# The last quarter of k for four row tiles: 32x32 blocks on VectorE in place of transposes on TensorE

## Chip, cores and metric

One Trainium2 chip, one core. The metric is device microseconds of one execution, lower is better. A core has TensorE (PE; its weight loads are listed as PEld), VectorE (DVE), ScalarE (ACT), GpSimd (POOL) and SyncE (SP), which here only issues transfers. Each engine works through its own list of instructions in order. SP's and GpSimd's transfers go to DMA queues.

## What is computed

```python
def reference(a, b, gamma, beta, eps):        # a, b: 2048 x 2048, float32
    x = np.matmul(a, b)
    mean = np.mean(x, axis=-1, keepdims=True)
    var = np.var(x, axis=-1, keepdims=True)
    normalized = (x - mean) / np.sqrt(var + eps)
    return (gamma * normalized + beta).astype(np.float32)
```

A product of two 2048×2048 matrices, then a layer norm over each row of the result.

## The kernel before

**Tiling.** A is cut into 16 row tiles i (or g) of 128 rows, k into 16 steps t of 128, B's columns into four quarters q of 512. One product `mm(i, q, t)` (line 139) multiplies A's transposed block (128×128, fp16) with a block of B (128×512, fp16) into one of the eight PSUM banks. TensorE needs A with k on the partitions, so every block of A has to be transposed. k is dealt to the steps so that four steps share a quarter c of k (512 values): value p·4 + t of quarter c lies on partition p of step 4c + t. B is loaded and kept in that order (`b_rows`, line 68), as is A's transposed tile `at[i]`, 128 × 16 steps × 128 (line 128).

**Loads of B.** `load_b(t, h)` (line 74) fetches half h of B's row tile t: 128 partitions × 1024 float32, 512 KB, into one of eight buffers. `cast_left` and `cast_right` (lines 79 and 84) turn a tile into fp16, one half of the columns on VectorE, the other on ScalarE. It is complete in SBUF as fp16 and is read by all row tiles.

**Two ways to transpose A.** Row tiles 0 to 3 go by pieces: 16 pieces n, piece n being row tile n mod 4 and quarter n // 4 of k (`pieces`, line 89). `load_first(n)` (line 91) fetches one with the rows on the partitions (128 × 512 float32, one transfer of 256 KB, 2 KB a row); `cast_first` (line 100) makes it fp16 on VectorE and reorders it; `turn_first` (line 105) transposes it on TensorE, four times 128×128, into a PSUM bank; `keep_first` (line 110) copies that to `at[g]` on VectorE. Row tiles 4 to 15 go by quadrants: `load_tile` (line 114) makes eight transfers of 64 KB, each filling 32 partitions with 32 rows r of each of the four blocks of 32 rows, and 128 values of k (512 bytes a run); `cast_tile` (line 122) makes fp16 on ScalarE, and `transpose_part` (line 130) turns 32×32 blocks on VectorE for one quarter of k, writing straight to `at[i]`.

**Order of the start.** The order of all engines is written out by hand (line 297). SP loads (lines 312 to 335): pieces 0 to 3 with B's left tiles 0 to 3, each piece of A one ahead of B's; the right tiles 0 to 3 with pieces 4 to 7; then B's left tiles 4 to 15, each of tiles 4 to 11 followed by one of the pieces 8 to 15; then B's right tiles 4 to 15, with row tile 4 in quadrants among the last of them.

TensorE computes row tiles 0 to 3 in four stages. The first quarter of k (t = 0 to 3, `K1 = 4`) is done for B's left half, then for the right half; the partial sums are put by in SBUF (`put_by`, line 150). Then the rest of k (t = 4 to 15) is done for the left half and the right half, and the partial sums are added (`add_up`, line 157). A half of four row tiles fills all eight banks, `left` or `right`; a transposed piece needs a bank too, so the eighth (`late`) joins the others once its bank is free of transposes. In the third stage (lines 428 to 445) step t keeps the piece before, casts the next, casts B's tile t + 1, and makes five products, four transposes and two products; when t = 12 is done, the late bank catches up on t = 4 to 12, and a closing loop (lines 446 to 451) takes t = 13, 14, 15 bank by bank and adds up. Then come row tiles 4 to 14 one by one (line 483) and the last one in narrower spans. The products of `warm_up` (line 303) only keep TensorE at work; nobody reads them.

Of the kernel before, what the change touches and what calls it, by code (L numbers as in the profile page):

```python
# [9 lines left out]
FP32 = mybir.dt.float32  # L10
FP16 = mybir.dt.float16
# [4 lines left out]
def kernel(  # L16
# [18 lines left out]
    nc = tc.nc  # L35
    P = 128
# [3 lines left out]
    n_kt = K // P  # L40
# [3 lines left out]
    G = 4  # L44
# [4 lines left out]
    firstp = ctx.enter_context(tc.tile_pool(name="firstp", bufs=4))  # L49
    first16 = ctx.enter_context(tc.tile_pool(name="first16", bufs=2))  # L50
    a16p = ctx.enter_context(tc.tile_pool(name="a16p", bufs=6))
# [17 lines left out]
    a_pieces = a.rearrange("(s r) (c q k) -> q c r s k", r=32, c=4, q=4)  # L69

    bnst, x_of, mv_of, rs_of, at = {}, {}, {}, {}, {}
    a_in, b_in, t_of, tile_in, part = {}, {}, {}, {}, {}

    def load_b(kt, h, queue=None):
        w = bigp.tile([P, NH], FP32, tag="big", name=f"w{kt}_{h}")
        (queue or nc.sync).dma_start(w, b_rows[kt // 4, kt % 4][:, ds(h * NH, NH)])
        b_in[kt, h] = w

    def cast_left(kt):
        w = b_in.pop((kt, 0))  # L80
        nc.vector.tensor_copy(b16[:, kt, 0:NB], w[:, 0:NB])
        nc.scalar.copy(b16[:, kt, NB:NH], w[:, NB:NH])

    def cast_right(kt):
        w = b_in.pop((kt, 1))
        nc.vector.tensor_copy(b16[:, kt, NH:NH + NB], w[:, 0:NB])
        nc.scalar.copy(b16[:, kt, NH + NB:N], w[:, NB:NH])
# [3 lines left out]
    def load_first(n):  # L91
        g, c = pieces[n]
        if n % 2 == 0:
            a_in[n + 1] = firstp.tile([P, 2, 4 * P], FP32, tag="first", name=f"f{g}_{c}")
            a_in[n] = a_in[n + 1][:, 0]
        else:
            a_in[n] = a_in[n][:, 1]
        nc.sync.dma_start(a_in[n], a[ts(g, P), ts(c, 4 * P)])

    def cast_first(n):  # L100
        h = first16.tile([P, P, 4], FP16, tag="h", name=f"h{n}")
        nc.vector.tensor_copy(h.rearrange("m p t -> m (p t)"), a_in[n])
        a_in[n] = h

    def turn_first(n):
        t_of[n] = psum.tile([P, 4, P], FP16, tag="c_ps", bufs=8, name=f"t_ps{n}")
        for t in range(4):
            nc.tensor.transpose(t_of[n][:, t, :], a_in[n][:, :, t], ident)

    def keep_first(n):  # L110
        g, c = pieces[n]
        nc.vector.tensor_copy(at[g][:, ds(4 * c, 4), :], t_of[n])  # L112

    def load_tile(i, h, queue):
        f = firstp.tile([P, 2, 4, P], FP32, tag="first", name=f"p{i}_{h}")
        for c in (0, 1):
            for q in range(4):
                queue.dma_start(  # L118
                    f[ds(32 * q, 32), c], a_pieces[q, 2 * h + c][:, ds(4 * i, 4)])
        tile_in[i, h] = f  # L120

    def cast_tile(i, h):
        a16 = a16p.tile([P, 2, 4, P], FP16, tag="a16", name=f"a{i}_{h}")
        nc.scalar.copy(a16, tile_in.pop((i, h)))  # L124
        tile_in[i, h] = a16
# [10 lines left out]
    def bank(i, q):  # L136
        x_of[i, q] = psum.tile([P, NB], FP32, tag="c_ps", bufs=8, name=f"ps_{i}_{q}")

    def mm(i, q, kt, lo=0, hi=n_kt):
        nc.tensor.matmul(  # L140
            x_of[i, q], at[i][:, kt, :], b16[:, kt, ds(q * NB, NB)],
            start=(kt == lo), stop=(kt == hi - 1),
        )
# [6 lines left out]
    def put_by(i, q):  # L150
        part[i, q] = xpool.tile([P, NB], FP32, tag="x_sb", name=f"x_{i}_{q}")
        if q % 2:
            nc.vector.tensor_copy(part[i, q], x_of[i, q])
        else:
            nc.scalar.copy(part[i, q], x_of[i, q])
# [141 lines left out]
    with tc.manual_schedule(engines=order):  # L297
# [5 lines left out]
        def warm_up(n):  # L303
            for _ in range(n):
                nc.tensor.matmul(w_ps, warm[:, 0:P], warm, start=True, stop=True)  # L305
# [3 lines left out]
            base=0, pattern=[[-1, P]], channel_multiplier=1,  # L309
        )  # L310
        K1 = 4
        load_first(0)
        for t in range(K1):
            if t + 1 < K1:
                load_first(t + 1)
            load_b(t, 0)
        for t in range(K1):
            load_b(t, 1)
# [2 lines left out]
        load_first(2 * K1 - 1)  # L321
        for t in range(K1, n_kt):
            load_b(t, 0)
            if K1 + t < n_kt:
                load_first(K1 + t)
        for t in range(K1, n_kt - 2):
            load_b(t, 1)
        load_tile(4, 0, nc.sync)
        for t in range(n_kt - 2, n_kt):
            load_b(t, 1)  # L330
        load_tile(4, 1, nc.sync)
        for h in (0, 1):
            load_tile(5, h, nc.sync)
# [6 lines left out]
        left = [(g, q) for g in range(G) for q in (0, 1)]  # L340
        right = [(g, q) for g in range(G) for q in (2, 3)]
        early, late = left[:-1], left[-1]
# [1 line left out]
            new_at(g)  # L344


        def step(t, gs):
            for g in gs:
                for q in (0, 1):
                    mm(g, q, t, 0, K1)  # L350

        warm_up(10)
        cast_first(0)
        turn_first(0)
        cast_first(1)
        warm_up(1)
        keep_first(0)
        turn_first(1)
        warm_up(2)
        keep_first(1)  # L360
        cast_left(0)
        for x in early[:4]:
            bank(*x)
        step(0, (0, 1))
        cast_first(2)
        turn_first(2)
        warm_up(2)
        keep_first(2)
        cast_left(1)
        for x in early[4:]:  # L370
            bank(*x)
        step(0, (2,))
        step(1, (0, 1))
        cast_first(3)
        turn_first(3)
        step(1, (2,))
        keep_first(3)
        bank(*late)
        step(0, (3,))
        step(1, (3,))  # L380
        cast_left(2)
        step(2, range(G))
        cast_left(3)
        for j, (g, q) in enumerate(left):
            mm(g, q, K1 - 1, 0, K1)
            put_by(g, q)
            if j == 3:
                cast_right(0)
        cast_right(1)


        early, late = right[:-1], right[-1]
# [13 lines left out]
        waits = list(range(K1))  # L406
        for j, (g, q) in enumerate(early):
            mm(g, q, K1 - 1, 0, K1)
            put_by(g, q)
            if j in (4, 6):  # L410
                n = K1 + j // 2
                turn_first(n)
                keep_first(n)
            if j in (1, 3, 5):
                mm(*late, waits.pop(0), 0, K1)
            if j == 2:
                cast_left(K1)
            if j == 5:
                cast_first(2 * K1)
        for t in waits:  # L420
            mm(*late, t, 0, K1)
        put_by(*late)
# [2 lines left out]
        early, late = left[:-1], left[-1]  # L425
        for g, q in early:
            bank(g, q)
        for t in range(K1, n_kt - 3):
            n = K1 + t
            if t > K1:  # L430
                keep_first(n - 1)
            if K1 < t and n < n_kt:
                cast_first(n)
            cast_left(t + 1)
            for g, q in early[:5]:
                mm(g, q, t, K1)
            if n < n_kt:
                turn_first(n)
            for g, q in early[5:]:
                mm(g, q, t, K1)  # L440
        bank(*late)
        for t in range(n_kt - 2, n_kt):
            cast_left(t)
        for t in range(K1, n_kt - 3):
            mm(*late, t, K1)
        for j, (g, q) in enumerate(left):
            for t in range(n_kt - 3, n_kt):
                mm(g, q, t, K1)
# [96 lines left out]
```

## Time and profile before

| | |
|---|---|
| median of 3 runs | 244.94 us (244.73 to 245.02) |
| the profiled execution, its own time | 244.94 us |
| its span in the profile | 243.2 us, mean granted TensorE clock 0.991 |
| DMA traffic | 52.66 MB, mean 217 GB/s |

The page's second part shows the span in 40 slices of 6.08 us. Digits are busy tenths; PEclk is the granted TensorE clock, DMA the mean busy share of 16 DMA engines:

```profile
PE   8899999999999999999999999999999999999960
PEld 3434554444444444444444444444444444446440
DVE  1657864894499999998999899998999895966962
ACT  2364434543325230461908255370917391020020
POOL 0000000000786599788866807693760000000011
PEclk9999999999999999999999999999999999999996
DMA  5999999995999768585675626473674222030405
GB/s 154 412 402 401 400 402 409 406 343 165 245 222 315 198 181 277 183 270 136 243 208 204 228 97 241 158 281 89 216 213 170 98 86 89 31 142 0 175 0 173
```

A column is one moment. The first nine columns, some 55 us, are the loading of B and of the first row tiles; the four stages of row tiles 0 to 3 end at 68.8 us.

### The profile page before, as it was taken

What the parts mean: (1) busy time and instruction counts of PE and PEld (TensorE: products, weight loads), DVE (VectorE), ACT (ScalarE), POOL (GpSimd) and SP (SyncE); (2) the same over time, 40 slices, a digit from 0 to 9 for tenths busy, and PEclk for the clock granted to TensorE, in tenths of its full rate; (3) what the DMA queues carried; (4) which work ended last, traced back from release to release, by engine and by line L of the source; (5) the groups of instructions that cost most, each with busy time, mean ns of one, the idle gap of its engine ahead of it and who ended that gap; (6) DMA issues with size and microseconds to landing.
All of it is one profiled execution on the core that took longest, in us unless ns stands there. A gap on an engine that the chain in (4) does not pass through costs nothing.

```text
span 243.2 us, 3383 instructions
## 1 busy us (share of the span) xinstructions
PE 232.3 (96%) x1135; PEld 108.3 (45%) x1135; DVE 198.3 (82%) x373; ACT 92.7 (38%) x165; POOL 89.4 (37%) x168
## 2 busy tenths in 40 slices
PE   8899999999999999999999999999999999999960
PEld 3434554444444444444444444444444444446440
DVE  1657864894499999998999899998999895966962
ACT  2364434543325230461908255370917391020020
POOL 0000000000786599788866807693760000000011
PEclk9999999999999999999999999999999999999996
DMA  5999999995999768585675626473674222030405
GB/s 154 412 402 401 400 402 409 406 343 165 245 222 315 198 181 277 183 270 136 243 208 204 228 97 241 158 281 89 216 213 170 98 86 89 31 142 0 175 0 173
DMA packets 22129, 52.66 MB, mean 217 GB/s; under 512 B 4448, under 2 KB 9056, under 8 KB 21856
## 3 DMA queue, kind: packets, MB, share of 16 engines
q1 hardware_dynamic: 16704, 41.74, 47.6%
q0 software_dynamic: 5120, 10.50, 16.6%
q10 hardware_dynamic: 288, 0.21, 0.3%
q8 instruction: 9, 0.15, 0.2%
q14 instruction: 8, 0.07, 0.1%
HBM read 35.65 MB, written 16.78 MB: 216 GB/s over the span
## 4 chain that ended last, share of the span: by engine, by line
PE 91%; DVE 3%; DMA 2%; SPq 0%; issue 0%; DVEq 0%
DMA w_0_109<-in_b_dram 2%; PE ps_0_2051 L140 1%; PE ps_1_1374 L140 1%; PE ps_0_998 L140 1%; PE ps_last_2337 L229 1%; PE ps_last_2318 L229 1%; PE ps_3_2233 L140 1%; PE ps_2_2215 L140 1%; PE ps_0_2178 L140 1%; PE ps_1_1966 L140 1%; PE ps_0_1943 L140 1%; PE ps_2_1870 L140 1%; PE ps_3_1770 L140 1%; PE ps_1_1728 L140 1%; PE ps_0_1705 L140 1%; PE ps_0_1589 L140 1%
## 5 line engine op out<-in xcount | busy, mean ns | idle before, releaser
L214 ACT ACTIVATE junk<-b_93 128x1024 f16<-128x1024 f16 x32 | 33.7, 1054 | 0.5
L118 POOL DMA_DIRECT2D p_0_232<-in_a_dram x8 | 4.9, 622 | 59.0 <-DMA w_1_199<-in_b_dram 59.0
L268 POOL TENSOR_TENSOR u_last_n<-u_last_n,gamma_b 128x128 f32<-128x128 f32 x1 | 0.5, 453 | 54.1 <-ACT u_last_n L267 54.1
L229 PEld LDWEIGHTS <-at_2050 128*128 128x128 f16 x96 | 8.8, 98 | 5.4
L140 PEld LDWEIGHTS <-at_412 128*128 128x128 f16 x64 | 6.1, 98 | 9.0 <-issue 2.1
L140 PEld LDWEIGHTS <-at_997 128*128 128x128 f16 x64 | 6.3, 98 | 7.5
L140 PEld LDWEIGHTS <-at_1350 128*128 128x128 f16 x64 | 6.3, 98 | 7.5
L140 PEld LDWEIGHTS <-at_1826 128*128 128x128 f16 x64 | 6.3, 98 | 7.5
L140 PEld LDWEIGHTS <-at_1942 128*128 128x128 f16 x64 | 6.3, 98 | 7.5
L140 PEld LDWEIGHTS <-at_988 128*128 128x128 f16 x64 | 6.3, 98 | 7.5
L140 PEld LDWEIGHTS <-at_1115 128*128 128x128 f16 x64 | 6.3, 98 | 7.5
L140 PEld LDWEIGHTS <-at_1466 128*128 128x128 f16 x64 | 6.3, 98 | 7.5
L140 PEld LDWEIGHTS <-at_1588 128*128 128x128 f16 x64 | 6.3, 98 | 7.6
L140 PEld LDWEIGHTS <-at_1704 128*128 128x128 f16 x64 | 6.2, 97 | 7.6
L140 PEld LDWEIGHTS <-at_837 128*128 128x128 f16 x64 | 6.2, 97 | 7.6
L140 PEld LDWEIGHTS <-at_1228 128*128 128x128 f16 x64 | 6.2, 97 | 7.6
L140 PEld LDWEIGHTS <-at_413 128*128 128x128 f16 x64 | 6.2, 98 | 7.6
L140 PEld LDWEIGHTS <-at_415 128*128 128x128 f16 x64 | 6.2, 98 | 6.7 <-DVE at_415 L112 0.6
L140 PEld LDWEIGHTS <-at_414 128*128 128x128 f16 x64 | 6.1, 98 | 6.6 <-DVE at_414 L112 0.6
L305 PE MATMUL w_ps<-warm 128*128 128x512 f16 x15 | 6.3, 565 | 1.2 <-DVE warm L298 1.2
L118 POOL DMA_DIRECT2D p_0_358<-in_a_dram x8 | 4.3, 550 | 8.0 <-ACT a_0_1608 L124 5.5
L118 POOL DMA_DIRECT2D p_0_394<-in_a_dram x8 | 4.3, 548 | 5.5 <-ACT a_0_1846 L124 5.5
(575 smaller groups left out, 644.0 us busy)
## 6 DMA issues: line engine op xcount, KB each, us to landing
gamma_b<-in_gamma_dram SPq DMA_DIRECT2D x1, 1024.0 KB, 7.1
beta_b<-in_beta_dram SPq DMA_DIRECT2D x1, 1024.0 KB, 11.3
f_0_106<-in_a_dram SPq DMA_DIRECT2D x2, 256.0 KB, 4.1
w_0_109<-in_b_dram SPq DMA_DIRECT2D x1, 512.0 KB, 5.7
f_0_111<-in_a_dram SPq DMA_DIRECT2D x2, 256.0 KB, 6.4
w_0_113<-in_b_dram SPq DMA_DIRECT2D x1, 512.0 KB, 6.7
w_0_116<-in_b_dram SPq DMA_DIRECT2D x1, 512.0 KB, 7.7
w_0_118<-in_b_dram SPq DMA_DIRECT2D x1, 512.0 KB, 8.2
```

The costliest lines, as they stand in the source:

```text
L118: queue.dma_start(f[ds(32 * q, 32), c], a_pieces[q, 2 * h + c][:, ds(4 * i, 4)])
L140: nc.tensor.matmul(x_of[i, q], at[i][:, kt, :], b16[:, kt, ds(q * NB, NB)], start=(kt == lo), stop=(kt == hi - 1),)
L214: nc.scalar.activation(junk, b16[:, kt, ds(h * NH, NH)], ActFn.Copy, accum_out=b_sum[:, h, kt:kt + 1])
L229: nc.tensor.matmul(x[:, 0:w], at[last][:, t, :], b16[:, t, ds(lo, w)], start=(t == 0), stop=(t == n_kt - 1))
L268: nc.gpsimd.tensor_tensor(y, y, gamma_b[:, ds(lo, w)], AluOp.mult)
L305: nc.tensor.matmul(w_ps, warm[:, 0:P], warm, start=True, stop=True)
```

## The change

Row tiles 0 to 3 get their last quarter of k (pieces 12 to 15) in the second way: four transfers of 64 KB into quadrants (`load_fourth`), a cast on ScalarE and a transpose by 32×32 blocks on VectorE (`turn_fourth`). Their loads stand where the pieces stood, behind B's left tiles 8 to 11. In the third stage the transposes on TensorE end with step 7; the late bank catches up after step 8, and steps 9 to 12 run over all eight banks, each turning one row tile's last quarter.

The first stage is written anew: B's left tile t now follows A's piece t instead of piece t + 1, and the order of casts, transposes, products and warm-ups is another (19 warm-up products for 15). The cast of piece 8 moves from the second stage into the third's first step.

```diff
+    def load_fourth(g):
+        if g % 2 == 0:
+            tile_in[g, 3] = firstp.tile([P, 2, 4, P], FP32, tag="first", name=f"p{g}_3")
+            tile_in[g + 1, 3] = tile_in[g, 3]
+        for q in range(4):
+            nc.sync.dma_start(
+                tile_in[g, 3][ds(32 * q, 32), g % 2], a_pieces[q, 3][:, ds(4 * g, 4)])
+
+    def turn_fourth(g):
+        a16 = a16p.tile([P, 4, P], FP16, tag="a16", name=f"a{g}_3")
+        nc.scalar.copy(a16, tile_in[g, 3][:, g % 2])
+        nc.vector.transpose(
+            at[g][:, ds(12, 4), :].rearrange("p t (j r) -> p j t r", r=32),
+            a16.rearrange("p j (k t) -> p j t k", t=4),
+        )
...
         K1 = 4
-        load_first(0)
         for t in range(K1):
-            if t + 1 < K1:
-                load_first(t + 1)
+            load_first(t)
             load_b(t, 0)
...
         for t in range(K1, n_kt):
             load_b(t, 0)
-            if K1 + t < n_kt:
+            if t < 2 * K1:
                 load_first(K1 + t)
+            elif t < 3 * K1:
+                load_fourth(t - 2 * K1)
...
-        cast_first(1)
-        warm_up(1)
-        keep_first(0)
-        turn_first(1)
-        warm_up(2)
-        keep_first(1)
-        cast_left(0)
...
+        warm_up(3)
+        for n in range(K1):
+            keep_first(n)
+            cast_left(n)
+            if n < K1 - 1:
+                cast_first(n + 1)
+            for x in early:
+                if x[0] == n:
+                    bank(*x)
+            todo = [
+                (g, q, t) for t in range(n + 1) for g, q in early
+                if g <= n and (g == n or t == n)
+            ]
+            if n == K1 - 1:
+                break
+            ahead = (2, 4, 6)[n]
+            for x in todo[:ahead]:
+                mm(*x, 0, K1)
+            if n == 0:
+                warm_up(2)
+            turn_first(n + 1)
+            for x in todo[ahead:]:
+                mm(*x, 0, K1)
+            if n < 2:
+                warm_up(2)
         bank(*late)
+        for g, q, t in todo[:K1 - 1]:
+            mm(g, q, t, 0, K1)
+        waits = list(range(K1))
+        for j, (g, q) in enumerate(early):
             mm(g, q, K1 - 1, 0, K1)
             put_by(g, q)
+            if j in (1, 3, 5):
+                mm(*late, waits.pop(0), 0, K1)
             if j == 3:
                 cast_right(0)
+        for t in waits:
+            mm(*late, t, 0, K1)
+        put_by(*late)
         cast_right(1)
...
-        for t in range(K1, n_kt - 3):
+        for t in range(K1, 2 * K1):
             n = K1 + t
             if t > K1:
                 keep_first(n - 1)
-            if K1 < t and n < n_kt:
-                cast_first(n)
+            cast_first(n)
             cast_left(t + 1)
             for g, q in early[:5]:
                 mm(g, q, t, K1)
-            if n < n_kt:
-                turn_first(n)
+            turn_first(n)
             for g, q in early[5:]:
                 mm(g, q, t, K1)
+        keep_first(3 * K1 - 1)
+        cast_left(2 * K1 + 1)
+        for g, q in early:
+            mm(g, q, 2 * K1, K1)
         bank(*late)
+        for t in range(K1, 2 * K1 + 1):
+            mm(*late, t, K1)
+        for t in range(2 * K1 + 1, n_kt - 3):
+            cast_left(t + 1)
+            turn_fourth(t - 2 * K1 - 1)
+            for g, q in left:
+                mm(g, q, t, K1)
         for t in range(n_kt - 2, n_kt):
             cast_left(t)
-        for t in range(K1, n_kt - 3):
-            mm(*late, t, K1)
```

More of the change, by code (lines that the diff above doesn't have):

```diff
@@ L344 @@
             new_at(g)
[L347 to L350, printed above, removed]
         warm_up(10)
@@ L354 @@
         turn_first(0)
-        cast_first(1)
-        warm_up(1)
-        keep_first(0)
-        turn_first(1)
-        warm_up(2)
-        keep_first(1)
-        cast_left(0)
[L362 to L377, printed above, removed]
-        bank(*late)
[L379 to L384, printed above, removed]
+        warm_up(3)
[23 more added lines that the diff above has]
+                warm_up(2)
+        bank(*late)
+        for g, q, t in todo[:K1 - 1]:
+            mm(g, q, t, 0, K1)
+        waits = list(range(K1))
+        for j, (g, q) in enumerate(early):
             mm(g, q, K1 - 1, 0, K1)
             put_by(g, q)
+            if j in (1, 3, 5):
+                mm(*late, waits.pop(0), 0, K1)
             if j == 3:
                 cast_right(0)
+        for t in waits:
+            mm(*late, t, 0, K1)
+        put_by(*late)
         cast_right(1)
@@ L417 @@
                 cast_left(K1)
-            if j == 5:
-                cast_first(2 * K1)
         for t in waits:
```

## The prediction

> **What bounds the kernel now.** I read the busy shares first, then busy time by stage, then the timeline of the stage that the change touches, then the transfers.
>
> ```profile
> span 243.2 us, 3383 instructions
> PE 232.3 (96%) x1135; PEld 108.3 (45%) x1135; DVE 198.3 (82%) x373; ACT 92.7 (38%) x165; POOL 89.4 (37%) x168
> ```
>
> TensorE is busy nearly throughout, so anything taken off it looks like a gain. By stage (length, then busy time of PE, PEld, DVE, ACT, POOL, granted clock, DMA share, GB/s):
>
> ```profile
> 24.96:42.78 17.82, 17.81 (x105) 8.91 (x104) 11.21 (x30) 6.52 (x12) 0.00 (x0) 1.00 1.03 404
> 42.78:47.96 5.18, 5.18 (x25) 2.35 (x24) 4.60 (x9) 2.55 (x5) 0.00 (x0) 1.00 1.03 410
> 47.96:68.84 20.88, 20.88 (x97) 9.39 (x96) 13.79 (x28) 7.49 (x11) 6.27 (x11) 1.00 0.95 252
> ```
>
> 24.96 to 42.78 us is the left half of B, steps t = 4 to 12, where the removed transposes sit. TensorE has no gap there, but neither have the transfers: share 1.03 at 404 GB/s. Two limits lie side by side. Which ends last is read where the stage ends:
>
> ```profile
> 31.07 0.43 DVE L81 CAST b_93<-w_0_148 128x512 f16<-128x512 f32 x1
> 33.01 0.43 DVE L81 CAST b_93<-w_0_152 128x512 f16<-128x512 f32 x1 [0.32 <-DMA w_0_152<-in_b_dram]
> ...
> 40.13 0.43 DVE L81 CAST b_93<-w_0_164 128x512 f16<-128x512 f32 x1 [0.52 <-DMA w_0_164<-in_b_dram]
> ...
> 41.41 0.43 DVE L81 CAST b_93<-w_0_166 128x512 f16<-128x512 f32 x1 [0.85 <-DMA w_0_166<-in_b_dram]
> 42.69 0.43 DVE L81 CAST b_93<-w_0_168 128x512 f16<-128x512 f32 x1 [0.85 <-DMA w_0_168<-in_b_dram]
> 42.78 0.81 PE L140 MATMUL ps_0_627<-b_93,at_412 128*128 128x512 f16 x3
> ```
>
> These casts start when their piece of B lands (VectorE sat idle for it). A 512 KB row tile of B alone takes 1.28 us (40.13 to 41.41 to 42.69); with a 256 KB piece of A between, 1.94 (31.07 to 33.01; 1.96 in the three steps after it), so such a piece of A costs 0.67. w_0_168 is the last left tile, t = 15. It is cast by 42.69 + 0.43 = 43.12. The closing loop takes t = 13, 14, 15 bank by bank: its first three products start at 42.78, and with 0.216 us between starts the third, the first to read t = 15, starts at 43.21. The margin is **0.09 us**. Everything behind it (5.18 of 5.18 us busy, then 20.88 of 20.88) is dense on TensorE, so a tile 15 that lands D later ends the kernel D − 0.09 later, however early TensorE is ready.
>
> **The change part by part.**
>
> Transposes on TensorE: 16 go. A step with them takes 1.73 us (timeline: t = 7 starts at 30.44, t = 8 at 32.17), seven products alone 7 × 0.216 = 1.51; a group of four costs 0.22, and four groups 0.88 us of TensorE. By the margin at most 0.09 of it can reach the end.
>
> Casts and copies: per piece VectorE loses a cast and a PSUM copy (0.43 + 0.42) and gains one 32×32 transpose of 128×512 f16, 0.69 (median of the rows for tiles 4 to 15). ScalarE gains one 128×512 cast, 0.62 by its casts of B. VectorE gains 4 × 0.16 us; ScalarE, busy 6.52 of 17.82, has room. The new wait: VectorE's transpose stands behind ScalarE's copy, and both stand behind the cast of t + 1. For g = 3 that is the cast of t = 13: landing + 0.62 + 0.62 + 0.69 = 1.93 us later. Products (3, ·, 12) wait for it, and behind them on TensorE the closing loop: two products of t = 12 and the loop's first two take 4 × 0.216 = 0.86, so the third could start 2.79 after tile 13's landing. Tile 15 lands 2.56 after tile 13 and is cast 0.43 later, at 2.99: the wait is hidden, by 0.2 us only, and what goes beyond that adds to the end.
>
> Product order: bank (3, 1) takes t = 4 to 8 after step 8 and then goes along. As many products as before; this gives step 9 1.08 us more time to receive tile 9.
>
> Head: B's first tile moves ahead of A's second piece, and four more warm-up products run (19 for 15). The bytes up to B's fourth tile are the same, so it lands at 12.58 as before. Following VectorE's new order by its durations (0.42 to 0.69), I get row tile 3's piece kept at about 13.7, the left products done at 17.0 (16.2 before), and the first right product at 17.05 against 16.77, since there the put-by copies and the cast of B on VectorE decide. That is 0.3 us late, a few tenths either way. Bounds: 0.1 early to 1 late (warm-ups at the early pitch of 0.43 that fail to fit into waits). TensorE spends it before the wait for tile 15, so it costs nothing there; without that cover it costs its 0.3.
>
> Loads: this decides. Pieces 12 to 15 were one transfer each of 256 KB in 2 KB runs; now each is four transfers of 64 KB in 512-byte runs, in the same places of SP's queue: one group ahead of each of B's tiles 9, 10, 11, 12. Twelve more issues at 0.31 to 0.43 us add 3.7 to 5.2 us to SP's time over four steps of about 2 us. The queue's own waits show eight transfers in flight: each of tile 4's small ones waits for the transfer eight issues before.
>
> ```profile
> SPq L118 <- DMA w_1_186<-in_b_dram: 1.8, 1, 1.8
> SPq L118 <- DMA w_1_188<-in_b_dram: 1.7, 1, 1.7
> ```
>
> By their order, any eight transfers of the new stretch hold at least one B tile and 448 KB of the rest, some 3 us of work; the shortest issue to landing of these small ones is 1.9. So the queue should not run dry, narrowly. The price of the bytes, by stretches in which only this 512-byte kind moves (from SP and GpSimd) and the transfers are saturated, against one with 2 KB and 4 KB runs:
>
> ```profile
> 25.00:35.00 10.00, 10.00 (x62) 5.07 (x61) 7.17 (x20) 3.33 (x7) 0.00 (x0) 1.00 1.04 402
> ...
> 57.00:59.20 2.20, 2.20 (x12) 1.02 (x11) 1.01 (x2) 0.62 (x2) 0.00 (x0) 1.00 0.47 89
> ...
> 63.20:66.00 2.80, 2.80 (x14) 1.27 (x13) 0.00 (x0) 0.16 (x1) 2.25 (x5) 1.00 1.15 221
> 67.00:70.00 3.00, 3.00 (x16) 1.35 (x14) 3.00 (x6) 0.20 (x1) 2.51 (x5) 1.00 1.22 226
> 70.00:72.00 2.00, 2.00 (x11) 0.90 (x10) 2.00 (x4) 1.05 (x1) 2.00 (x5) 1.00 1.01 218
> ```
>
> Full share, half the rate. At 221 GB/s 256 KB takes 1.19 us for 0.67: **0.52 more a piece, 2.1 in four**. Upper bound: where tile 4's first 512 KB stood in SP's queue before. B's tile landed at 52.91, two more and these 512 KB by 59.18: 6.27 − 2 × 1.28 = 3.71, or 1.86 a piece, 1.19 more, 4.75 in four. Part of that is a dry queue (89 GB/s at share 0.47), as only small transfers followed; here a B tile follows each group. Lower bound: no more than now, 0. I take the saturated rate and an eighth of the way to the upper row for stragglers: D = 2.1 + 0.3 = 2.4.
>
> [...]
>
> The same stall leaves TensorE idle in pieces of 0.5 to 1.5 us between 39 and 45. [...]
>
> **Sum.** D − 0.09 = 2.4 − 0.1 = +2.3 us. The profiled execution took 244.94 us (span 243.2 and 1.7 around it), which is also the median of the runs: 244.94 + 2.3 = **247.2**.
>
> **Rivals.** *Small runs cost nothing*: D = 0, tile 15 lands as before, and only the margin is gained: 244.85. For it: 512-byte runs may move under cover of B's long ones, since several transfers are in flight; against it, the saturated stretches. It decides while D stays under 0.6. 7%. *The 0.88 us come out whole*, not slower: 244.94 − 0.88 = 244.06. It needs tile 15 to land 0.8 earlier, hence fewer bytes ahead of it or gaps to close; the share is 0.99 to 1.04 from 5 us on and the bytes are equal. 3%. *The queue runs dry*: eight in flight are too few as their size falls, the upper row holds, D = 4.75: 249.6. For it: SP's issue time per step, 5 × 0.31 to 0.43 = 1.55 to 2.15 us, is near the step's own. 15%. *No VectorE path*: that the transposes stay on TensorE is excluded by the diff.
>
> **How the numbers follow.** Forecast 75%: D between 1.5 and 3.6, 246.3 to 248.5, single value 247.2. The range goes below to D = 0.95, 245.8, and above to 249.4, which takes in most of the dry queue; what lies outside (the two rivals that are not slower, the worst of the dry queue) is some 2 in 10. What a measurement can tell from no change is 0.2%, 0.49 us: slower takes in the forecast and the dry queue, 0.90; within it lies the first rival, 0.07; faster the second, 0.03.
>
> **What would show it.** Landings of B's left tiles 9 to 12 at 2.4 to 2.6 us for 1.95, then 1.28 again; tile 15 cast at about 45.1; a gap on TensorE ahead of the first product of t = 15; the stages from there on as long as before; GB/s about 315 (768 KB in 2.5 us) between 33 and 41. The step on the transfers is wrong if tiles 9 to 12 keep their 1.95, and the step on the margin if TensorE is late for tile 15. The prediction fails on its sign if tile 15 lands by 43.

## The result and the profile after

The changed kernel takes 249.05 us (median of 4 runs, 248.1 to 249.66) against 244.98 for the kernel before; the ratio is 1.0164, 95% interval 1.013 to 1.0198. That is 4.07 us more, where 2.3 were forecast. The profiled execution took 249.66 us, 4.72 above the profiled execution of before.

The page of the changed kernel, span and busy time:

```profile
span 247.8 us, 3370 instructions
## 1 busy us (share of the span) xinstructions
PE 232.6 (94%) x1123; PEld 107.0 (43%) x1123; DVE 198.2 (80%) x369; ACT 95.0 (38%) x169; POOL 89.2 (36%) x168
```

TensorE works as long as before (232.6 for 232.3 us) in a span 4.6 longer: it waits. Where, by stage, with the same columns as before (third stage, its closing loop, fourth stage):

```profile
24.32:46.35 22.03, 17.60 (x89) 7.73 (x88) 10.93 (x25) 8.51 (x15) 0.00 (x0) 1.00 1.02 305
46.35:51.75 5.40, 5.34 (x25) 2.33 (x24) 4.76 (x10) 2.47 (x4) 0.00 (x0) 1.00 1.02 404
51.75:72.61 20.86, 20.86 (x97) 9.38 (x96) 12.64 (x25) 6.80 (x11) 4.73 (x8) 1.00 0.93 264
```

The fourth stage is as long as before (20.86 for 20.88) and without a gap. The third began 0.64 us earlier than before and ended 3.6 later; the transfers in it fell from 404 to 305 GB/s. VectorE's casts of B's left tiles, in the timeline, show why:

```profile
31.13 0.43 DVE L81 CAST b_93<-w_0_148 128x512 f16<-128x512 f32 x1 [0.45 <-DMA w_0_148<-in_b_dram]
34.45 0.43 DVE L81 CAST b_93<-w_0_155 128x512 f16<-128x512 f32 x1 [2.38 <-DMA w_0_155<-in_b_dram]
37.47 0.43 DVE L81 CAST b_93<-w_0_161 128x512 f16<-128x512 f32 x1 [2.59 <-DMA w_0_161<-in_b_dram]
40.56 0.43 DVE L81 CAST b_93<-w_0_168 128x512 f16<-128x512 f32 x1 [1.22 <-DMA w_0_168<-in_b_dram]
42.69 0.43 DVE L81 CAST b_93<-w_0_174 128x512 f16<-128x512 f32 x1 [0.24 <-DMA w_0_174<-in_b_dram]
...
46.53 0.43 DVE L81 CAST b_93<-w_0_180 128x512 f16<-128x512 f32 x1 [0.37 <-DMA w_0_180<-in_b_dram]
```

Tiles 8 to 12 land 3.32, 3.02, 3.09 and 2.13 us apart in place of 1.90 to 1.98; tile 15 (w_0_180) at 46.53, 3.84 later than before. The closing loop ends 3.79 later (its successor starts at 51.75 for 47.96): tile 15's delay less the margin. Ahead of it TensorE stands still for each of tiles 9 to 12 (line, then the wait and who ended it):

```profile
34.93 0.38 PE L156 MATMUL ps_0_641<-b_93,at_424 128*128 128x512 f16 x1 [0.30 <-DVE b_93 L81]
37.95 0.38 PE L156 MATMUL ps_0_641<-b_93,at_424 128*128 128x512 f16 x1 [1.12 <-DVE b_93 L81]
41.04 0.38 PE L156 MATMUL ps_0_641<-b_93,at_424 128*128 128x512 f16 x1 [1.21 <-DVE b_93 L81]
43.17 0.38 PE L156 MATMUL ps_0_641<-b_93,at_424 128*128 128x512 f16 x1 [0.24 <-DVE b_93 L81]
...
45.91 0.39 PE L156 MATMUL ps_0_647<-b_93,at_427 128*128 128x512 f16 x1 [0.68 <-DVE at_427 L133]
...
76.05 1.04 PE L156 MATMUL ps_0_994<-b_93,at_833 128*128 128x512 f16 x4 [0.69 <-DVE at_833 L147]
```

The fifth line is the wait for the last piece's transpose. Four products start from there (45.91, 46.14, 46.35, 46.57); the next one, which could start at 46.79, reads tile 15, whose cast ends at 46.96, so the wait costs nothing, by 0.2 us. The last line was not foreseen: row tile 4's own last quarter of k comes 0.69 us late, at 76.05. Together 3.79 + 0.69 = 4.48 of the span's 4.6.

SP's queue in the timeline (start, time taken, how many):

```profile
21.47 0.33 SPq L76 DMA_DIRECT2D w_0_148<-in_b_dram  x1
22.14 4.12 SPq L127 DMA_DIRECT2D p_3_150<-in_a_dram  x4
26.66 0.35 SPq L76 DMA_DIRECT2D w_0_155<-in_b_dram  x1
27.91 4.01 SPq L127 DMA_DIRECT2D p_3_150<-in_a_dram  x4
32.01 0.38 SPq L76 DMA_DIRECT2D w_0_161<-in_b_dram  x1
```

Tile 9 (w_0_155) is issued at 26.66 and tile 10 at 32.01; before the change they went out at 23.71 and 27.18. SP's four small issues take 4 us (4.12 and 4.01), as each waits for the completion of the transfer eight issues before: in the trace SP's 128 transfers use eight completion semaphores (the signals that a transfer has landed; numbers 100, 102, 104, 105 and 107 to 110) and take them in turn, and GpSimd's 160 use eight others (111 to 118). Two of SP's waits, each for the B tile eight issues before (total, times, longest):

```profile
SPq L127 <- DMA w_0_138<-in_b_dram: 0.9, 1, 0.9
SPq L127 <- DMA w_0_141<-in_b_dram: 1.3, 1, 1.3
```

Two readings are open at this point: the bytes move slowly (the forecast's term), or the queue holds too few of them. The stretches in which the small transfers move, with the columns of the stages:

```profile
28.00:41.00 13.00, 10.41 (x55) 4.76 (x53) 4.70 (x11) 3.34 (x6) 0.00 (x0) 1.00 1.01 236
33.00:41.00 8.00, 5.41 (x24) 2.21 (x23) 1.99 (x4) 2.19 (x4) 0.00 (x0) 1.00 0.99 244
```

The DMA share is still about 1, at little more than half the rate of before (403 GB/s at 1.03 from 28 to 41 us): mostly slow, and hardly dry.

### The profile page after: what moved, and what is told of

Same layout as the page of the kernel before. It is cut to its first block, busy times and chain, and to the rows that moved or that the text cites. A ratio compares the mean times of both kernels' runs of the same rounds, so it can differ in the third digit from the quotient of the medians.

```text
span 247.8 us, 3370 instructions
## 1 busy us (share of the span) xinstructions
PE 232.6 (94%) x1123; PEld 107.0 (43%) x1123; DVE 198.2 (80%) x369; ACT 95.0 (38%) x169; POOL 89.2 (36%) x168
## 4 chain that ended last, share of the span: by engine, by line
PE 66%; DMA 25%; DVE 4%; SPq 1%; ACT 1%; issue 0%; DVEq 0%; ACTq 0%
DMA w_1_200<-in_b_dram 5%; DMA f_2_143<-in_a_dram 4%; DMA w_0_118<-in_b_dram 3%; DMA f_1_131<-in_a_dram 3%; DMA p_3_150<-in_a_dram 3%; DMA w_0_180<-in_b_dram 2%; DMA w_0_168<-in_b_dram 2%; DMA w_1_213<-in_b_dram 2%; DMA p_1_215<-in_a_dram 2%; PE ps_2_2211 L156 1%; PE ps_3_2112 L156 1%; PE ps_0_2047 L156 1%; PE ps_1_1962 L156 1%; PE ps_2_1866 L156 1%; PE ps_3_1766 L156 1%; PE ps_0_1701 L156 1%
## 5 line engine op out<-in xcount | busy, mean ns | idle before, releaser
L118 POOL DMA_DIRECT2D p_0_244<-in_a_dram x8 | 4.7, 599 | 63.9 <-ACT a_0_859 L140 63.9
L321 PE MATMUL w_ps<-warm 128*128 128x512 f16 x19 | 7.0, 512 | 1.2 <-DVE warm L314 1.2
L118 POOL DMA_DIRECT2D p_0_370<-in_a_dram x8 | 4.3, 550 | 8.0 <-ACT a_0_1604 L140 5.5
L156 PE MATMUL ps_0_641<-b_93,at_424 128*128 128x512 f16 x12 | 4.4, 378 | 2.9 <-DVE b_93 L81 2.9
```

Of the source, the lines that this page charges most:

```text
L118: queue.dma_start(f[ds(32 * q, 32), c], a_pieces[q, 2 * h + c][:, ds(4 * i, 4)])
L156: nc.tensor.matmul(x_of[i, q], at[i][:, kt, :], b16[:, kt, ds(q * NB, NB)], start=(kt == lo), stop=(kt == hi - 1),)
```

## Experiments

The times are medians beside runs of the kernel before on the same chip (244.8 to 244.9); "tile 15" is the start of its cast on VectorE in the profile, 42.69 in the kernel before and 46.53 in the changed one; it is read from one execution of each kernel. All kernels but the last two replace only the transfers in `load_fourth` (diffs against the changed kernel, where nothing else is said); the rest of it stays.

**Whole pieces.** What do the transfers cost, and what do 1.5 us of lead on TensorE bring?

```diff
-        for q in range(4):
-            nc.sync.dma_start(
-                tile_in[g, 3][ds(32 * q, 32), g % 2], a_pieces[q, 3][:, ds(4 * g, 4)])
+        nc.sync.dma_start(
+            tile_in[g, 3][:, g % 2].rearrange("p j k -> p (j k)"),
+            a[ts(g, P), ds(12 * P, 4 * P)])
```

> Each of the four last pieces is fetched whole, one transfer of 256 KB in 2 KB rows over 128 partitions, into the same tile; ScalarE's cast and VectorE's transposes run on it unchanged, so the transposed blocks of the last quarter hold other values. Main theory (the transfers alone cost the time, and TensorE's readiness is worth at most the 0.09 us margin): B's tile 15 lands at 42.7 as before, 244.9 us within 0.3. Rival (the 0.88 us of transposes and the 0.64 us that TensorE gained in the head come out): 243.4 to 244.1. Rival (the VectorE path itself delays): 247 or more.

Measured 244.62 us, ratio 0.9992 (0.9981 to 1.0002); tile 15 at 42.19. Busy times from 28 to 41 us in its profile, ending in granted clock, DMA share and GB/s:

```profile
28.00:41.00 13.00, 13.00 (x69) 6.03 (x66) 6.96 (x16) 6.50 (x12) 0.00 (x0) 1.00 1.03 405
```

The transfers run at the old rate and the whole loss is gone, with ScalarE's casts and VectorE's transposes in place: they cost nothing here. That is narrow. TensorE stood 0.48 us for the last piece's transpose:

```profile
41.57 13.70 PE L156 MATMUL ps<-b,at 128*128 128x512 f16 x61 [0.48 <-DVE at L133]
```

Four products on, it had to wait for tile 15 all the same (cast from 42.19 to 42.62). And four groups of transposes fewer and an earlier head bring no more than a gain that the interval doesn't tell from none.

**One transfer, short runs.** The run length alone.

```diff
+        nc.sync.dma_start(
+            tile_in[g, 3][:, g % 2],
+            a.rearrange("(s p) (c k) -> c p s k", p=P, k=P)[12 + g][:, ds(0, 4)])
```

> The same bytes in 512-byte runs, but as one transfer of 256 KB per piece that fills all 128 partitions (four row blocks of another part of A, so the last quarter holds other values). Theory of the runs (a 512-byte run costs twice its bytes): tiles 9 to 12 land 2.5 us apart, D about 2.1, 247 us, or the whole 249. Theory of the count (eight transfers in flight, whatever their size, starve the queue): 244.9. Theory of the quadrant (32 partitions at a time are the brake): 244.9.

Measured 245.47, ratio 1.0023 (1.0012 to 1.0034), tile 15 at 43.43. Beside whole pieces that is 1.24 us of delay, 0.31 a piece, and 0.85 us of time. The theory of the runs, the forecast's, falls: it asked for 2.1 or more of delay.

**Four transfers, all partitions.** The count, without quadrants.

```diff
+        for q in range(4):
+            nc.sync.dma_start(
+                tile_in[g, 3][:, g % 2, q], a[ts(q, P), ds((12 + g) * P, P)])
```

> The same bytes in 512-byte runs, in four transfers of 64 KB per piece, each over all 128 partitions with one run each (other columns of A, so the last quarter holds other values). Theory of the runs: 247 to 249. Theory of the count: 247 to 249 too. Theory of the quadrant: 244.9. Beside the run with one transfer, the difference is the count alone.

Measured 247.94, ratio 1.0137 (1.0095 to 1.0178), tile 15 at 46.13. Same bytes, same runs, same partitions as the run before; only four transfers for one, and 2.5 us more. The same stretch, first for one transfer, then for four:

```profile
28.00:41.00 13.00, 12.90 (x69) 5.99 (x67) 6.09 (x14) 5.40 (x10) 0.00 (x0) 1.00 1.06 377
```

```profile
28.00:41.00 13.00, 11.61 (x64) 5.58 (x63) 5.24 (x12) 4.13 (x7) 0.00 (x0) 1.00 0.89 283
```

The share falls to 0.89: there is too little in flight. This is a dry queue. SP's issues in this kernel, third and fourth group, tell a second reason beside the semaphores:

```profile
31.63 0.40 SPq L76 DMA_DIRECT2D w<-in_b_dram  x1
32.13 1.80 SPq L127 DMA_DIRECT2D p<-in_a_dram  x4
34.02 0.38 SPq L76 DMA_DIRECT2D w<-in_b_dram  x1
34.44 1.97 SPq L127 DMA_DIRECT2D p<-in_a_dram  x4
```

Five issues take 2.4 to 2.5 us, most of it SP's own time for issuing (the single issues beside them take 0.38 to 0.40 each), while a step of the kernel before took 1.9 to 2.0. So the count of transfers costs in two ways, by the semaphores in the first two groups (4.89 and 2.81 us for four issues) and by SP's pace behind them; no run here separates the two.

**Quadrants, long runs.**

```diff
+        for q in range(4):
+            nc.sync.dma_start(
+                tile_in[g, 3][ds(32 * q, 32), g % 2].rearrange("p j k -> p (j k)"),
+                a[ds(g * P + 32 * q, 32), ds(12 * P, 4 * P)])
```

> Four transfers of 64 KB per piece into 32 partitions each, but in 2 KB runs (32 rows of the piece; the last quarter holds other values). Theory of the runs: 244.9. Theory of the count: 247 to 249. Theory of the quadrant: 247 to 249.

Measured 249.06, ratio 1.0181 (1.0158 to 1.0205), tile 15 at 46.61: as the changed kernel itself (249.05), with runs four times as long. In quadrants the run length makes no difference to the time. Its stretch from 28 to 41 us has 231 GB/s at share 0.87, for 236 at 1.01 in the change, so in quadrants the share alone doesn't tell slow from dry.

**Pairs in quadrants.** If the count is all, half as many transfers of double size should give nearly everything back.

```diff
+        for q in (2 * (g % 2), 2 * (g % 2) + 1):
+            nc.sync.dma_start(
+                tile_in[g, 3][ds(32 * q, 32)].rearrange("p g j k -> p (g j) k"),
+                a_pieces[q, 3][:, ds(8 * (g // 2), 8)])
```

> The changed kernel's own data, with each quadrant's transfer made for two row tiles at once: 8 transfers of 128 KB in place of 16 of 64 KB, two at each of the four places in SP's queue. Still 512-byte runs, still 32 partitions. Theory of the count (eight completion semaphores in turn, so eight transfers in flight whatever their size): any eight hold over 1.5 MB again, B's tiles 9 to 12 are issued in time, 245.3 to 245.8, near the run with one transfer per piece. Theory of the runs or of the quadrant: 247 to 249.

Measured 251.62, ratio 1.0283 (1.0261 to 1.0306), tile 15 at 49.28: slower than the change by 2.6 us. The theory of the count alone falls here. The same stretch of this kernel:

```profile
28.00:41.00 13.00, 10.15 (x56) 4.72 (x55) 4.08 (x10) 2.99 (x5) 0.00 (x0) 1.00 1.11 219
```

Share 1.11: this queue is full, and everything in it, B's tiles too, moves at 219 GB/s.

**Pairs over all partitions.** Count, size and run length of the run before; only the partitions differ.

```diff
+        for j in (0, 2):
+            nc.sync.dma_start(
+                tile_in[g, 3][:, g % 2, ds(j, 2)],
+                a.rearrange("(s p) (c k) -> c p s k", p=P, k=P)[12 + g][:, ds(j, 2)])
```

> The count and size of the run with pairs (8 transfers of 128 KB, two at each place, 512-byte runs), but each over all 128 partitions (other rows of A, so the last quarter holds other values). Theory of the partitions (a transfer into few partitions moves at a fraction of the rate, and B's tiles queue behind it): 245.3 to 246, against 251.6 for the pairs in quadrants. Theory of the count: above 247, as eight transfers are more than four.

Measured 245.34, ratio 1.0009 (0.9986 to 1.0033), tile 15 at 43.10:

```profile
28.00:41.00 13.00, 12.78 (x69) 5.95 (x66) 6.33 (x14) 5.73 (x10) 0.00 (x0) 1.00 1.06 376
```

376 GB/s for 219, and 6.3 us. So 8 transfers of 128 KB are not too many, and filling 32 partitions at a time is a brake of its own.

**Half of the partitions.** 64 at a time.

```diff
+        for c in (0, 1):
+            nc.sync.dma_start(
+                tile_in[g, 3][ds(64 * (g % 2), 64), c],
+                a.rearrange("(s p) (c k) -> c p s k", p=P, k=P)[
+                    12 + g // 2 * 2 + c][ds(64 * (g % 2), 64), ds(0, 4)])
```

> 8 transfers of 128 KB again, each over 64 partitions: at the places of row tiles 0 and 2 both fill partitions 0 to 63, at the others both 64 to 127 (other values in the last quarter). If the rate goes by the number of partitions of one transfer, 64 are twice as good as 32: 247 to 248.5. [...]

Measured 252.19, ratio 1.029 (1.0235 to 1.0345), tile 15 at 50.40. The same stretch:

```profile
28.00:41.00 13.00, 8.83 (x49) 4.12 (x48) 3.45 (x9) 2.09 (x4) 0.00 (x0) 1.00 1.11 212
```

212 GB/s at share 1.11, and 219 at 1.11 with the pairs in quadrants: 64 partitions are no better than 32. The theory that the rate goes by the number of partitions of one transfer falls, which asked for 247 to 248.5.

**Pairs, quadrants crossed.** One quadrant of each half at each place (diff against the pairs in quadrants).

```diff
-        for q in (2 * (g % 2), 2 * (g % 2) + 1):
+        for q in (g % 2, g % 2 + 2):
```

> The run with pairs, its own data, with only the order of the quadrants changed: 0 and 2 at the first place, 1 and 3 at the second, in place of 0, 1 and 2, 3. If the two quadrants of one half of the partitions are in each other's way, this gives most of the loss back: 246 to 248.5. If a quadrant is slow by itself, 251 to 252 as before. 245 or less would make it as good as the kernel before.

Measured 250.61, ratio 1.0215 (1.015 to 1.0281), tile 15 at 48.73, 225 GB/s. It recovers 1.0 us of the pairs' 6.7. The order of the quadrants matters little: a quadrant beside one of the other half is nearly as slow.

**From GpSimd's queue.** Its completion semaphores are its own (111 to 118 in the trace of the change), so SP's eight stay with large transfers, and SP is spared the twelve more issues. Once with the changed kernel's quadrants, once with the four transfers over all partitions (`nc.gpsimd` for `nc.sync`).

> The changed kernel's 16 transfers of 64 KB, issued from GpSimd's queue in place of SP's, which has semaphores of its own; they go out as soon as their buffers are free, some 20 to 29 us. Theory of the count as a limit on transfers in flight: SP's eight are all large again, so tile 15 lands about a microsecond late at most, 245.2 to 246. Theory of the count as a fixed price that each transfer costs the DMA engines: 248 to 249, as in SP's queue.

> The run with four transfers of 64 KB over all partitions (247.9 from SP's queue), issued from GpSimd's queue, whose completion semaphores are its own. Theory that the limit of eight transfers in flight on SP's semaphores starves the queue: 245.2 to 246.2. Theory of a fixed price per transfer on the DMA engines: 247.5 to 249.

Measured 250.17, ratio 1.0213 (1.0166 to 1.0261), and 247.93, ratio 1.0121 (1.0065 to 1.0177). Both expectations of the main theory missed in time, the second instructively:

```profile
28.00:41.00 13.00, 11.55 (x62) 5.47 (x61) 6.20 (x15) 5.87 (x11) 2.98 (x6) 1.00 1.03 387
```

In the second kernel the queue no longer runs dry (387 GB/s at share 1.03, for 283 at 0.89 with the same transfers in SP's queue), and tile 15's cast starts at 43.28 for 46.13. So a fixed price per transfer on the DMA engines is not what made it 46.13; what made it is in SP's queue, the eight in flight and SP's pace. But GpSimd issued eight of the 16 at 20.1 to 24.7 us, past the B tiles that stood in SP's queue ahead of them, and tiles 7 and 8 came late instead (cast at 30.58 and 33.43, for 29.14 and 31.07 in the kernel before): TensorE waits 0.49 and 0.96 us for them and then runs without a gap from 33.9 us until row tile 4, whose last quarter is late by 0.59. With quadrants tile 15 stays at 46.24, as the brake of the partitions predicts.

1.3 us of the second time have nothing to do with the stage. Behind its last work GpSimd runs a `DRAIN` at the end of the program. With 160 transfers in GpSimd's queue it lasted 5.33 us in the kernel before, in the changed one and in the four transfers over all partitions from SP's queue; with 176, these from GpSimd's, it lasted 6.64. The span ended 0.8 us behind it in all four. The rows for four transfers over all partitions, from SP's queue and then from GpSimd's (the longest of three is the third of the numbers in ns; then the start of the first, which is that one, and of the last):

```profile
L561 POOLq DRAIN  x3: 40/102/5330, 240.4 to 246.3; - x3
L561 POOLq DRAIN  x3: 46/102/6640, 238.4 to 245.6; - x3
```

Without these 1.3 us the second kernel would stand at an estimated 246.6, 1.3 below the same transfers in SP's queue, and the quadrants, with 176 transfers too and by the same 1.3, at 248.9, where the change is (their runs spread from 248.5 to 251.4).

**The two halves of the change.** The new first stage alone, in the kernel before; and the changed kernel with the old first stage.

```diff
 # kernel before
-        load_first(0)
         for t in range(K1):
-            if t + 1 < K1:
-                load_first(t + 1)
+            load_first(t)
             load_b(t, 0)
...
-        step(0, (0, 1))
...
+        for n in range(K1):
+            keep_first(n)
+            cast_left(n)
...
```

> The kernel before with the changed first stage and its order of loads alone; the last pieces stay on TensorE. Main theory (tile 15's landing ends the left half, TensorE's 0.64 us from the head don't come out): 244.8, within 0.2 of the kernel before. Rival (TensorE bounds the left half): 244.3.

> The changed kernel with the first stage and its loads as they were before. Main theory: the head is hidden by the wait for tile 15, so 248.5 to 249.5, as the whole change. Rival (the new head has a share in the loss): below 248.

Measured 244.67, ratio 0.999 (0.998 to 1.0), and 249.06, ratio 1.0176 (1.0151 to 1.02). The head alone gains at most a few tenths; the last quarter's new way alone costs the whole, and by the whole pieces that is its loads.

No version here is clearly faster than the kernel before. The transfers of a piece in one view:

| transfers of a piece | partitions each | runs | queue | tile 15 | time, us |
|---|---|---|---|---|---|
| 1 of 256 KB (whole) | 128 | 2 KB | SP | 42.19 | 244.62 |
| 1 of 256 KB | 128 | 512 B | SP | 43.43 | 245.47 |
| 2 of 128 KB | 128 | 512 B | SP | 43.10 | 245.34 |
| 4 of 64 KB | 128 | 512 B | SP | 46.13 | 247.94 |
| 4 of 64 KB | 128 | 512 B | GpSimd | 43.28 | 247.93 |
| 4 of 64 KB (the change) | 32 | 512 B | SP | 46.53 | 249.05 |
| 4 of 64 KB | 32 | 2 KB | SP | 46.61 | 249.06 |
| 4 of 64 KB | 32 | 512 B | GpSimd | 46.24 | 250.17 |
| 2 of 128 KB, crossed | 32 | 512 B | SP | 48.73 | 250.61 |
| 2 of 128 KB | 32 | 512 B | SP | 49.28 | 251.62 |
| 2 of 128 KB | 64 | 512 B | SP | 50.40 | 252.19 |

The two brakes don't add up. Among the rows with four transfers of 64 KB in 512-byte runs, tile 15 is cast at 43.28 with neither (all partitions, GpSimd's queue), at 46.13 with SP's queue alone, at 46.24 with the quadrants alone, and at 46.53 with both, in the change: either alone makes nearly the whole delay. GpSimd's transfers also went out earlier, so this holds for where tile 15 lands and not for the times.

## Why the prediction was right, and where its size was off

**What bounds the stage: right.** Tile 15's landing ends the left half. Delay 3.84 less 0.09 gives 3.75, and the loop ended 3.79 later; TensorE's lead of whole pieces and of the new head didn't come out (244.62 and 244.67 for 244.9). TensorE's idle pieces ahead of tiles 9 to 12, 0.24 to 1.21 us where 0.5 to 1.5 were forecast, came at a granted clock of 1.00. The 0.88 us of transposes were worth nothing, as said.

**VectorE and ScalarE: right.** The wait for the last piece's transpose was hidden, and by as little as worked out: the closing loop's third product could have started 0.2 us before tile 15 was cast.

**The head: wrong in sign, without effect.** I expected the first right product 0.3 us later; it came at 16.14, 0.63 earlier than before, because row tile 3's piece was kept by 12.9 and not 13.7. It went into the wait for tile 15, as the prediction said it would. The early pitch of 0.43 us in the forecast's bounds is that of the warm-up products which start the kernel before: their weight loads come 0.43 apart from 1.60 to 4.58 us; the products from 7.88 us on start 0.216 apart.

**The price of the bytes: the term that was mis-sized.** "At 221 GB/s 256 KB takes 1.19 us for 0.67: 0.52 more a piece, 2.1 in four", with 0.3 for stragglers, D = 2.4. It measured 3.84. The rate was read rightly from rows in which only transfers of this kind move, but put down to the 512-byte runs. All those transfers also fill 32 partitions each, and by the runs that is what counts: with runs of 512 bytes over 128 partitions the price was 0.31 a piece and not 0.52; with quadrants, 2 KB runs cost as much as short ones. And the price was put on the pieces alone, with B's tiles beside them at 1.28 us as before. It fell on everything: for 33 to 41 us 315 GB/s were forecast, and 244 were measured at a full share. A small misreading beside it: the three steps after 1.94 were 1.96, 1.98 and 1.90, not 1.96 each, which leaves the 0.67 as it is.

**"So the queue should not run dry, narrowly": wrongly argued, and in the change itself not what decides.** It set 3 us of work in flight against the shortest issue-to-landing time in the trace, 1.9 us, which is that of a small transfer with no B tile ahead of it any more. In the changed kernel the first eight small transfers took 4.3 to 9.3 us to land (median 6.7). Against such times eight in flight, of which seven may be small, are too few: four transfers over all partitions lose 2.5 us against one of the same runs (247.94 and 245.47), at share 0.89. In quadrants, taking the small transfers out of SP's queue brought tile 15 only 0.3 us earlier (46.24 for 46.53).

**How near the numbers came: in part luck.** The measured D of 3.84 and the 249.05 us lie outside what the forecast gave at 75%, 1.5 to 3.6 and 246.3 to 248.5. They lie inside the stated range because its upper end was drawn to take in most of the dry queue. That rival's 249.6 came nearest, but from a row at share 0.47; the changed kernel's stretch stands at 1.01.

**The stages behind: not quite.** They were to be as long as before, with everything shifted alike. The transfers shifted more than TensorE: row tile 4's second half was cast at 72.42 for 66.15, 6.3 later, when TensorE was 3.8 later. That used up the 1.7 us by which its transposes had been early (ready 69.7, needed 71.4) and added 0.69.

**Open.** Why four quadrants of 64 KB (249.05) lose less than two of 128 KB (251.62): the share is 1.01 at 236 GB/s in the one and 1.11 at 219 in the other, and no run tells why. And why B's tiles themselves slow down beside quadrants. At the 221 GB/s of the forecast's row 1 MB of quadrants would cost an estimated 2.1 us more than whole pieces (4 × 0.52). In pairs tile 15 came 7.1 later (49.28 for 42.19). And why 64 partitions at a time are no better than 32 (212 and 219 GB/s): no run here shows it.

## What to carry to other kernels

When the transfers and TensorE are both full in a stage, find the last product that waits for a landing, and by how much it is free: that margin is all that work taken off TensorE can bring. Price a transfer by rows that agree with it in every respect, run length, partitions filled, size and queue, because a rate read from transfers that differ in three of them can't be assigned to one. Where completion semaphores go round, count transfers, not bytes: cutting one into four takes large ones out of flight and costs the issuing engine's time, here 2.5 us over four places.

## What the runs showed of the hardware that was not expected

Transfers of 128 KB into 32 or 64 partitions at a time brought the whole queue, the 128-partition transfers in it too, down to 212 to 225 GB/s at a DMA share of 1.11; as many bytes over 128 partitions ran at 376. Runs of 512 bytes over 128 partitions cost 0.31 us in 256 KB beside 2 KB runs. The share of busy time alone doesn't tell these apart: 1.03 at 403 GB/s in the kernel before, 1.11 at 219 with pairs. Sixteen more transfers issued by GpSimd went with a `DRAIN` at the end of the program that was 1.3 us longer (6.64 for 5.33), and the span with it.
